# Seven block products, and both halves of an operand in one 512-column matmul, for the MLP up-projection of an encoder block

## The chip, the cores and the metric

The kernel runs on one core of a Trainium2 chip. The metric is the device time of one execution in microseconds (us). The engines in the text are PE (TensorE, with PEld for its weight loads), DVE (VectorE), ACT (ScalarE), POOL (GpSimd) and SP (SyncE, which here issues the DMAs that are not POOL's).

## The reference

All tensors are float32, one batch, 512 tokens, width 2048.

```python
D_MODEL = 2048
SEQ = 512
D_FF = 4 * D_MODEL
...
Block:  h = x + W_out( sig(gA) * P_A(NAtt(xn)) + sig(gB) * P_B(BiGDN(xn)) ),  xn = RMSNorm(x)
        h = h + W_down( relu(RMSNorm(h) W_up)^2 )
        y = RMSNorm_final(h)
```

The change lies in the second of these lines: `W_up` takes the 2048 values of a token to 8192, a relu and a square follow, and `W_down` takes them back to 2048.

## The kernel before, in words

**Arithmetic.** TensorE multiplies in fp32r, a rounded form of float32. So every operand is split in two: `hi` is the value rounded by ACT (a cast, L89 for a weight unit, L94 elsewhere), `lo` is what the rounding left, which DVE subtracts (L90, L95). `unit_mm` then issues three matmuls for each 128x128 piece of a weight: `hi`·`hi` (L115), `hi`·`lo` (L116) and `lo`·`hi` (L117), each over all 512 tokens, so 512 columns.

**Units.** A weight comes in units of 128 partitions by 1024 (512 KB): eight 128x128 pieces that share an output block of 128 rows, for one half of the 2048 inputs. `load_raw` (L82, on SP) brings a unit into one of four `raw` buffers, and `load_unit` splits it into `wh_...` and `wl_...`, three buffers each.

**Stages on PE.** The input projection, the two attention branches and their gates come first. Then come w_out (16 output blocks `m`; `ps_b<-mh,wh_wo` in the trace), the MLP up-projection (64 output blocks of two units; `ps_b<-hh,wh_up`), and the MLP down-projection (`ps_b<-hih,wh_dn`). The last matmuls of the kernel are over 256 columns (L926 to L928).

**The activations of the up-projection.** After each output block of w_out, DVE adds the residual (L855, tile `xr`), ACT and DVE split the result (`hh` L861, `hl` L862), and the sum of its squares goes on (`sqh` L822, `sacc` L826). `stat` and `rstd_bcast` make the reciprocal norm of each token from it: eight one-column matmuls (L833, L834), a row of small DVE instructions (L142, L122 to L127, L145), one matmul. That norm is not applied to `hh` but, as `rB`, at the eviction of the up-projection.

**The up-projection.** For each `m` of 64: two units, 48 matmuls into one PSUM bank; DVE L872 (relu, times `rB`), ACT L873 (square), and SP stores the block to DRAM (`hidD`, L874). From `m` = 41 on, `load_hid` brings eleven finished blocks back (`hr`, L843) and splits them (`hih`, `hil`) for the down-projection. PSUM has seven banks for all of this.

**Order.** The program is written in the order of the stages, but a scheduler places the instructions of each engine by priorities and costs, and each engine works its own queue off in order. Pools give the tiles their buffers: a DMA into a buffer waits until the last reader of the tile before it in that buffer is done, and it waits at the head of SP's queue, with all later DMAs of SP behind it. `big` tiles have 48 buffers of 2 KB, `ev` tiles four.

Of the kernel before, what the change touches and what calls it, by code (L numbers as in the profile page):

```python
# [19 lines left out]
T = 512  # L20
# [7 lines left out]
NPUMP = 4  # L28
# [21 lines left out]
def tile_hybrid_block(  # L50
# [34 lines left out]
    def load_unit(src, name):  # L85
        raw = load_raw(src, name)
        hi = st.tile([128, 1024], F32R, tag="wh", name=f"wh_{name}", bufs=3)
        lo = st.tile([128, 1024], F32R, tag="wl", name=f"wl_{name}", bufs=3)
        S_.copy(out=hi, in_=raw)  # L89
        V.tensor_tensor(out=lo, in0=raw, in1=hi.bitcast(F32), op=ALU.subtract)  # L90
        return hi, lo
# [692 lines left out]
    with ExitStack() as p1:  # L784
# [3 lines left out]
        def bank():  # L788
            return mmp.tile([128, T], F32, tag="mm", name="ps_b")
# [30 lines left out]
        def sumsq(src, m, nm, ts=slice(0, T)):  # L820
            sq = tp.tile([128, T], F32, tag="sq", name=f"sq{nm}", bufs=2)
            S_.activation(out=sq[:, ts], in_=src[:, ts], func=AF.Square)  # L822
            if m == 0:
                V.tensor_copy(out=acc, in_=sq)
            elif m < 15:
                V.tensor_tensor(out=acc[:, ts], in0=acc[:, ts], in1=sq[:, ts], op=ALU.add)  # L826
            return sq
# [15 lines left out]
            nc.sync.dma_start(out=raw, in_=hidD[k])  # L843
            return split(raw, big(f"hih{k}"), big(f"hil{k}"))

        hT = []
        with ExitStack() as p5:
            hq = p5.enter_context(tc.tile_pool(name="hq", bufs=1, side="right", reuse_waits="tile"))
            for m in range(16):
                ps = bank()  # L850
                xr = ev(f"xr{m}")
                nc.sync.dma_start(out=xr, in_=xT[:, m, :])
                for u in range(2):
                    unit_mm(ps, load_unit(wout[m, u], f"wo{m}_{u}"), mix, 8 * u, u == 0, u == 1)
                V.tensor_tensor(out=xr, in0=ps, in1=xr, op=ALU.add)  # L855
                nc.sync.dma_start(out=hTD[m], in_=xr)
                if m < 8:
                    hh, hl = big(f"hh{m}"), big(f"hl{m}")
                else:
                    hh, hl = hq.tile([128, T], F32R, name=f"hh{m}"), hq.tile([128, T], F32R, name=f"hl{m}")  # L860
                S_.activation(out=hh, in_=xr, func=AF.Copy, scale=nlw_s[:, m : m + 1])  # L861
                V.scalar_tensor_tensor(out=hl, in0=xr, scalar=nlw_s[:, m : m + 1], in1=hh.bitcast(F32), op0=ALU.mult, op1=ALU.subtract)  # L862
                hT.append((hh, hl))
                sq = sumsq(xr, m, f"h{m}")
            tasks.append(stat("h", sq))
            hid0 = []
            for m in range(64):
                ps = bank()
                for u in range(2):
                    unit_mm(ps, load_unit(wup[m, u], f"up{m}_{u}"), hT, 8 * u, u == 0, u == 1)  # L870
                r = ev(f"ur{m}")
                V.scalar_tensor_tensor(out=r, in0=ps, scalar=0.0, in1=rB, op0=ALU.max, op1=ALU.mult)  # L872
                S_.activation(out=r, in_=r, func=AF.Square)  # L873
                nc.sync.dma_start(out=hidD[m], in_=r)  # L874
                if m >= 40 and m % 2 == 1 and len(hid0) < 11:
                    hid0.append(load_hid(len(hid0)))

        hp = p1.enter_context(tc.tile_pool(name="hp", bufs=1, side="right", reuse_waits="tile"))
        Ha = hp.tile([128, 16, T], F32, name="Ha")
# [141 lines left out]
```

## Time and profile before

| | |
|---|---|
| time before, median of 2 runs | 2957.06 us (2955.55 to 2958.57) |
| the profiled execution, first to last instruction (its span, and its own time) | 2960.0 us |
| mean granted TensorE clock of that execution | 0.995 |
| busy share of PE, PEld, DVE, ACT, POOL | 98%, 81%, 46%, 29%, 1% |
| PE's first and last start on up-projection matmuls | 1534.5 and 2243.9 us |
| its PE matmuls | 3 x 1024 |

The time of an execution is that of its slowest core, and there is one core. The profiled execution is one more execution than the two timed; durations below are from it. A busy share is an average over the whole span: what an engine does in one stage is read from that stage.

### The profile page before, as it was taken

Reading aid. Unit: us, or ns where it says so; the run is one execution under the profiler, and the core shown is the slowest. Engines: PE = TensorE matmul, PEld = TensorE weight load, DVE = VectorE, ACT = ScalarE, POOL = GpSimd, SP = SyncE. Lnnn points to the kernel's source line nnn. Section 1 sums busy time; section 2 is a strip of 40 time slices with the busy share of each in tenths; the row PEclk is TensorE's granted clock in tenths of the full one; section 3 lists DMA queues with packets and bytes.
Section 4 is the critical chain, followed back from the end, with each engine's and each line's share of the span. In section 5 each row is a group of like instructions: output and inputs, shape, how many; then the busy total and the mean of one; then the engine's idle time right before and its main releaser. Section 6 shows DMA issues by size and latency. Waiting matters only on the chain.

```text
span 2960.0 us, 33906 instructions
## 1 busy us (share of the span) xinstructions
PE 2913.1 (98%) x13432; PEld 2397.5 (81%) x13432; DVE 1365.7 (46%) x2071; ACT 872.6 (29%) x1333; POOL 24.7 (1%) x66
## 2 busy tenths in 40 slices
PE   8999999999999999999999999999999999999998
PEld 6778788888788888888888888888888888888887
DVE  6888769744554443444342222223333242332333
ACT  6444322233233333222222222222223131221322
POOL 0000000000000000000000000000000000000000
PEclk9999999999999999999999999999999999999999
DMA  7556653655532223443433333334336243342322
GB/s 228 185 182 186 207 185 118 219 153 171 183 114 96 91 85 132 160 155 117 148 125 114 123 119 118 120 118 136 128 129 230 94 155 100 107 143 94 113 100 86
DMA packets 170847, 411.95 MB, mean 139 GB/s; under 512 B 34368, under 2 KB 46720, under 8 KB 170688
## 3 DMA queue, kind: packets, MB, share of 16 engines
q1 hardware_dynamic: 170016, 407.69, 41.7%
q0 software_dynamic: 672, 2.10, 0.3%
q8 instruction: 105, 1.72, 0.2%
q14 instruction: 54, 0.44, 0.0%
HBM read 350.84 MB, written 58.88 MB: 138 GB/s over the span
## 4 chain that ended last, share of the span: by engine, by line
PE 72%; DVE 0%; SPq 0%; DMA 0%; ACT 0%; issue 0%; DVEq 0%; POOL 0%
PE ps_b L115 20%; PE ps_b L116 20%; PE ps_b L117 20%; PE ps_mm L117 4%; PE ps_mm L115 3%; PE ps_mm L116 3%; PE ps_ax L676 0%; PE ps_b L926 0%; PE ps_b L927 0%; PE ps_b L928 0%; DVE Ha L906 0%; PE ps_ax L137 0%; PE ps_ax L690 0%; PE ps_ax L692 0%; PE ps_ax L691 0%; PE ps_ax L657 0%
## 5 line engine op out<-in xcount | busy, mean ns | idle before, releaser
L115 PE MATMUL ps_mm<-xh,wh_in 128*128 128x512 f32 x1416 | 567.3, 401 | 3.4 <-ACT wh_in L89 3.4
L117 PE MATMUL ps_mm<-xh,wl_in 128*128 128x512 f32 x1416 | 560.6, 396 | 1.3 <-DVE wl_in L90 1.3
L116 PE MATMUL ps_mm<-xl,wh_in 128*128 128x512 f32 x1416 | 560.0, 395 | 0.0
L115 PE MATMUL ps_b<-hh,wh_up 128*128 128x512 f32 x1024 | 402.0, 393 | 0.0
L117 PE MATMUL ps_b<-hh,wl_up 128*128 128x512 f32 x1024 | 401.7, 392 | 0.0
L116 PE MATMUL ps_b<-hl,wh_up 128*128 128x512 f32 x1024 | 401.5, 392 | 0.0
L116 PE MATMUL ps_b<-hil,wh_dn 128*128 128x512 f32 x992 | 385.8, 389 | 0.0
L117 PE MATMUL ps_b<-hih,wl_dn 128*128 128x512 f32 x992 | 385.7, 389 | 0.0
L115 PE MATMUL ps_b<-hih,wh_dn 128*128 128x512 f32 x992 | 385.7, 389 | 0.0
L117 PEld LDWEIGHTS ps_mm<-xh,wl_in 128*128 128x128 f32 x1416 | 267.8, 189 | 62.3 <-DVE wl_in L90 2.6
L115 PEld LDWEIGHTS ps_mm<-xh,wh_in 128*128 128x128 f32 x1416 | 267.7, 189 | 59.1 <-ACT wh_in L89 4.0
L116 PEld LDWEIGHTS ps_mm<-xl,wh_in 128*128 128x128 f32 x1416 | 267.8, 189 | 54.7 <-issue 0.2
L89 ACT CAST wh_in<-raw_in 128x1024 fp32r<-128x1024 f32 x177 | 186.0, 1051 | 414.5 <-PE ps_mm L116 325.7
L89 ACT CAST wh_up<-raw_up 128x1024 fp32r<-128x1024 f32 x128 | 134.6, 1052 | 529.1 <-PE ps_b L116 300.0
L90 DVE TENSOR_TENSOR wl_up<-raw_up,wh_up 128x1024 fp32r<-128x1024 f32 x128 | 156.8, 1225 | 274.5 <-ACT wh_up L89 274.5
L90 DVE TENSOR_TENSOR wl_in<-raw_in,wh_in 128x1024 fp32r<-128x1024 f32 x177 | 216.2, 1222 | 121.4 <-ACT wh_in L89 114.8
L89 ACT CAST wh_dn<-raw_dn 128x1024 fp32r<-128x1024 f32 x124 | 130.9, 1055 | 477.1 <-PE ps_b L116 461.5
L90 DVE TENSOR_TENSOR wl_dn<-raw_dn,wh_dn 128x1024 fp32r<-128x1024 f32 x124 | 151.9, 1225 | 244.4 <-ACT wh_dn L89 244.1
L116 PEld LDWEIGHTS ps_b<-hl,wh_up 128*128 128x128 f32 x1024 | 192.2, 188 | 43.8 <-issue 0.2
L115 PEld LDWEIGHTS ps_b<-hh,wh_up 128*128 128x128 f32 x1024 | 192.2, 188 | 43.6 <-issue 0.2
L117 PEld LDWEIGHTS ps_b<-hh,wl_up 128*128 128x128 f32 x1024 | 192.1, 188 | 43.4
L116 PEld LDWEIGHTS ps_b<-hil,wh_dn 128*128 128x128 f32 x992 | 186.2, 188 | 38.9 <-DVE hil L95 0.2
(307 smaller groups left out, 3203.1 us busy)
## 6 DMA issues: line engine op xcount, KB each, us to landing
raw_in<-in_win SPq DMA_DIRECT2D x177, 512.0 KB
raw_up<-in_wup SPq DMA_DIRECT2D x128, 512.0 KB
raw_dn<-in_wdn SPq DMA_DIRECT2D x124, 512.0 KB
raw_wo<-in_wout SPq DMA_DIRECT2D x32, 512.0 KB
hidD<-ur SPq DMA_DIRECT2D x64, 256.0 KB
hr<-hidD SPq DMA_DIRECT2D x64, 256.0 KB
gD<-g SPq DMA_DIRECT2D x32, 256.0 KB
raw_pa<-in_wpa SPq DMA_DIRECT2D x16, 512.0 KB
```

The lines of the kernel that those rows point to most:

```text
L89: S_.copy(out=hi, in_=raw)
L90: V.tensor_tensor(out=lo, in0=raw, in1=hi.bitcast(F32), op=ALU.subtract)
L115: PE.matmul(ps, hi[:, w], rh, start=first and kk == 0, stop=False)
L116: PE.matmul(ps, hi[:, w], rl, start=False, stop=False)
L117: PE.matmul(ps, lo[:, w], rh, start=False, stop=last and kk == 7)
```

## The change

The 64 output blocks are taken in 32 pairs (`m0`, `m1` = `m0` + 8), and the weight of a pair is a 2x2 matrix of units: `A11` and `A12` (two halves of the inputs, block `m0`), `A21` and `A22` (block `m1`). The activations are a 2x2 matrix as well: two halves of the inputs by two halves of the tokens, 256 each. The eight block products of such a pair are replaced by seven, of sums and differences of the blocks. `XT1` to `XT4` are made of the activations once, from the differences `TR`; `X11`, `X21`, `X22` are plain blocks. The weight sums are made for every pair: `S1` = `A21` + `A22`, `S3` = `A21` + `A11`, `S2` = `S1` + `A11`, `S4` = `S2` + `A12`.

An activation block of 256 tokens has its `hi` and its `lo` half side by side in one tile of 512 columns. A product is then eight times (one 512-column matmul with the weight's `hi`, one 256-column matmul with its `lo`, L912 and L913). Each half of the bank holds a part of the result, and they are added afterwards on DVE (`fold`, L899; L950 and L955 read both).

`S1` and `S3` are made by DMAs: SP loads `A21` into a `sum` tile (L922, L925), and POOL issues a second DMA that adds the other unit to it (L923, L926, `accum_op`). `S2` and `S4` are DVE additions (L934; L957, and L936 in the first pair). The `sum` tiles have four buffers, and the pool that holds them stands where the `TR` tiles stood before.

```diff
-        hT = []
+        p7 = ExitStack()
+        bq = p7.enter_context(tc.tile_pool(name="bq", bufs=8, side="right", reuse_waits="tile"))
+
+        def operand(src, name):
+            t = bq.tile([128, T], F32R, tag="B2", name=name) if name.startswith("X11") else big(name)
+            split(src, t[:, 0:256], t[:, 256:512])
+            return t
+
+        lo_t, hi_t = slice(0, 256), slice(256, 512)
+        XS = {}
...
+            TR = []
+            xs = []
+            for n, m in enumerate(m for j in range(8) for m in (j, j + 8)):
...
-                if m < 8:
-                    hh, hl = big(f"hh{m}"), big(f"hl{m}")
+                sq = sumsq(xr, n, f"h{m}")
+                S_.activation(out=xr, in_=xr, func=AF.Copy, scale=nlw_s[:, m : m + 1])
+                xs.append(xr)
+                if n % 2 == 0:
+                    XS["11", m] = operand(xr[:, lo_t], f"X11_{m}")
                 else:
-                    hh, hl = hq.tile([128, T], F32R, name=f"hh{m}"), hq.tile([128, T], F32R, name=f"hl{m}")
-                S_.activation(out=hh, in_=xr, func=AF.Copy, scale=nlw_s[:, m : m + 1])
-                V.scalar_tensor_tensor(out=hl, in0=xr, scalar=nlw_s[:, m : m + 1], in1=hh.bitcast(F32), op0=ALU.mult, op1=ALU.subtract)
-                hT.append((hh, hl))
-                sq = sumsq(xr, m, f"h{m}")
+                    j = n // 2
+                    x0, x1 = xs[n - 1], xs[n]
+                    XS["21", j] = operand(x1[:, lo_t], f"X21_{j}")
+                    XS["22", j] = operand(x1[:, hi_t], f"X22_{j}")
+                    t = tr.tile([128, 4, 256], F32, tag="tr", name=f"TR{j}")
+                    V.tensor_tensor(out=t[:, 0], in0=x0[:, lo_t], in1=x0[:, hi_t], op=ALU.subtract)
+                    V.scalar_tensor_tensor(out=t[:, 1], in0=t[:, 0], scalar=-1.0, in1=x1[:, hi_t], op0=ALU.mult, op1=ALU.subtract)
+                    V.tensor_tensor(out=t[:, 2], in0=x1[:, hi_t], in1=x0[:, hi_t], op=ALU.subtract)
+                    V.scalar_tensor_tensor(out=t[:, 3], in0=t[:, 1], scalar=-1.0, in1=x1[:, lo_t], op0=ALU.mult, op1=ALU.subtract)
+                    TR.append(t)
             tasks.append(stat("h", sq))
-            hid0 = []
-            for m in range(64):
-                ps = bank()
-                for u in range(2):
-                    unit_mm(ps, load_unit(wup[m, u], f"up{m}_{u}"), hT, 8 * u, u == 0, u == 1)
-                r = ev(f"ur{m}")
-                V.scalar_tensor_tensor(out=r, in0=ps, scalar=0.0, in1=rB, op0=ALU.max, op1=ALU.mult)
-                S_.activation(out=r, in_=r, func=AF.Square)
-                nc.sync.dma_start(out=hidD[m], in_=r)
-                if m >= 40 and m % 2 == 1 and len(hid0) < 11:
-                    hid0.append(load_hid(len(hid0)))
+            for o, e in (("T2", 1), ("T1", 0), ("T3", 2), ("T4", 3)):
+                for j in range(8):
+                    XS[o, j] = operand(TR[j][:, e], f"X{o}_{j}")
+            def sums(name, bufs=4):
+                return sm.tile([128, 1024], F32, tag="sum", name=name, bufs=bufs)
...
+            def fold(t):
+                V.tensor_tensor(out=t[:, lo_t], in0=t[:, lo_t], in1=t[:, hi_t], op=ALU.add)
+                return t[:, lo_t]
...
+            def product(ps, w, o, first=False):
+                hi, lo = w
+                for j in range(8):
+                    x = XS[o, j]
+                    c = slice(j * 128, (j + 1) * 128)
+                    PE.matmul(ps, hi[:, c], x, start=first and j == 0, stop=False, skip_group_check=True)
+                    PE.matmul(ps[:, 0:256], lo[:, c], x[:, 0:256], start=False, stop=j == 7, skip_group_check=True)
+                    if j % NPUMP == NPUMP - 1:
+                        pump()
+
+            for i in range(32):
+                m0 = i // 8 * 16 + i % 8
+                m1 = m0 + 8
+                a11 = load_raw(wup[m0, 0], f"A11_{i}")
+                s1, s3 = sums(f"S1_{i}"), sums(f"S3_{i}")
+                nc.sync.dma_start(out=s1, in_=wup[m1, 0])
+                G.dma_start(out=s1, in_=wup[m1, 1], accum_op=ALU.add)
+                a12 = load_raw(wup[m0, 1], f"A12_{i}")
+                nc.sync.dma_start(out=s3, in_=wup[m1, 0])
+                G.dma_start(out=s3, in_=wup[m0, 0], accum_op=ALU.add)
+                a22 = load_raw(wup[m1, 1], f"A22_{i}")
+                a, b, c = (bank() for _ in range(3))
+                t1, t5, u2 = et(f"t1_{i}"), et(f"t5_{i}"), et(f"u2_{i}")
+                r0, r1 = ev(f"ur{m0}"), ev(f"ur{m1}")
+                s2, s4 = sums(f"S2_{i}"), sums(f"S4_{i}")
+                product(a, wsplit(a11, f"A11_{i}"), "11", True)
+                S_.copy(out=t1, in_=a)
+                V.tensor_tensor(out=s2, in0=s1, in1=a11, op=ALU.add)
+                if i == 0:
+                    V.tensor_tensor(out=s4, in0=s2, in1=a12, op=ALU.add)
+                    product(c, wsplit(s4, f"S4_{i}"), "22", True)
+                    S_.copy(out=t5, in_=c)
+                    product(a, wsplit(a12, f"A12_{i}"), "21")
+                product(b, wsplit(s2, f"S2_{i}"), "T2", True)
+                V.tensor_tensor(out=u2, in0=b, in1=t1, op=ALU.add)
+                product(c, wsplit(s1, f"S1_{i}"), "T1", i > 0)
+                if i == 0:
+                    V.tensor_tensor(out=t5, in0=c, in1=t5, op=ALU.subtract)
+                else:
+                    S_.copy(out=t5, in_=c)
+                    product(a, wsplit(a12, f"A12_{i}"), "21")
+                f1 = et(f"f1_{i}")
+                S_.copy(out=f1[:, lo_t], in_=a[:, hi_t])
+                V.tensor_tensor(out=f1[:, lo_t], in0=a[:, lo_t], in1=f1[:, lo_t], op=ALU.add)
+                V.scalar_tensor_tensor(out=r0[:, lo_t], in0=f1[:, lo_t], scalar=0.0, in1=rB[:, lo_t], op0=ALU.max, op1=ALU.mult)
+                product(b, wsplit(s3, f"S3_{i}"), "T3")
+                V.tensor_tensor(out=t5, in0=b, in1=t5, op=ALU.add)
+                V.tensor_tensor(out=t5, in0=t5, in1=t1, op=ALU.add)
+                V.scalar_tensor_tensor(out=r1[:, hi_t], in0=fold(t5), scalar=0.0, in1=rB[:, hi_t], op0=ALU.min, op1=ALU.mult)
+                if i > 0:
+                    V.tensor_tensor(out=s4, in0=s2, in1=a12, op=ALU.add)
+                    product(c, wsplit(s4, f"S4_{i}"), "22")
+                V.tensor_tensor(out=u2, in0=c, in1=u2, op=ALU.add)
+                V.scalar_tensor_tensor(out=r0[:, hi_t], in0=fold(u2), scalar=0.0, in1=rB[:, hi_t], op0=ALU.max, op1=ALU.mult)
+                S_.activation(out=r0, in_=r0, func=AF.Square)
+                nc.sync.dma_start(out=hidD[m0], in_=r0)
+                product(b, wsplit(a22, f"A22_{i}"), "T4")
+                V.tensor_tensor(out=t1, in0=b, in1=t1, op=ALU.add)
+                V.scalar_tensor_tensor(out=r1[:, lo_t], in0=fold(t1), scalar=0.0, in1=rB[:, lo_t], op0=ALU.min, op1=ALU.mult)
+                S_.activation(out=r1, in_=r1, func=AF.Square)
+                nc.sync.dma_start(out=hidD[m1], in_=r1)
+            hid0 = [load_hid(k) for k in range(16)]
+        p7.close()
```

The pairs after the first take their products in the order `A11`, `S2`, `S1`, `A12`, `S3`, `S4`, `A22`; the first pair takes `S4` and `A12` right after `A11`. Below, a number behind a tile's name is the pair (and one more that keeps tiles of a name apart).

DVE in the middle of the up-projection, before (the splits of two blocks' units, the eviction of the block before):

```order
L90 TENSOR_TENSOR wl_up20_0_13316<-raw_up20_0_13313,wh_up20_0_13315 128x1024
L90 TENSOR_TENSOR wl_up20_1_13346<-raw_up20_1_13343,wh_up20_1_13345 128x1024
L872 SCALAR_TENSOR_TENSOR ur19_13308<-ps_b_13247,rB_79 128x512
L90 TENSOR_TENSOR wl_up21_0_13381<-raw_up21_0_13378,wh_up21_0_13380 128x1024
L90 TENSOR_TENSOR wl_up21_1_13411<-raw_up21_1_13408,wh_up21_1_13410 128x1024
```

and after, from the addition that makes the next pair's `S2` to the split of that `S2`; `raw_A11`, `wl_A22` and the like are units, `t1`, `t5`, `u2`, `f1` and `ur` are evictions:

```order
L934 TENSOR_TENSOR S2_12_14420<-S1_12_14402,raw_A11_12_14400 128x1024
L95 TENSOR_TENSOR wl_S4_11_14351<-S4_11_14236,wh_S4_11_14350 128x1024
L957 TENSOR_TENSOR S4_12_14421<-S2_12_14420,raw_A12_12_14406 128x1024
L95 TENSOR_TENSOR wl_A22_11_14376<-raw_A22_11_14225,wh_A22_11_14375 128x1024
L950 TENSOR_TENSOR f1_11_14321<-ps_b_14227,f1_11_14321 128x256
L951 SCALAR_TENSOR_TENSOR ur19_14233<-f1_11_14321,rB_79 128x256
L953 TENSOR_TENSOR t5_11_14231<-ps_b_14228,t5_11_14231 128x512
L954 TENSOR_TENSOR t5_11_14231<-t5_11_14231,t1_11_14230 128x512
L95 TENSOR_TENSOR wl_A11_12_14423<-raw_A11_12_14400,wh_A11_12_14422 128x1024
L899 TENSOR_TENSOR t5_11_14231<-t5_11_14231 128x256
L959 TENSOR_TENSOR u2_11_14232<-ps_b_14229,u2_11_14232 128x512
...
L95 TENSOR_TENSOR wl_S2_12_14445<-S2_12_14420,wh_S2_12_14444 128x1024
```

Left out in the last of these are one L955 and one L899, both of 256 columns. What was two splits and an eviction for a block is now seven splits, two additions and thirteen smaller instructions for a pair. The addition that makes `S2` of the next pair (its first operand is the `S1` that a POOL DMA completes) stands right behind this pair's split of `S3`, and ahead of the splits of this pair's `S4` and `A22`.

SP in the same place, before and after (`hidD` is the store of a finished block):

```order
L82 DMA raw_up20_0_13313<-in_wup 128x1024
L82 DMA raw_up20_1_13343<-in_wup 128x1024
L874 DMA hidD_94<-ur17_13178 128x512
L82 DMA raw_up21_0_13378<-in_wup 128x1024
L82 DMA raw_up21_1_13408<-in_wup 128x1024
```

```order
L82 DMA raw_A11_12_14400<-in_wup 128x1024
L82 DMA raw_A12_12_14406<-in_wup 128x1024
L922 DMA S1_12_14402<-in_wup 128x1024
L962 DMA hidD_94<-ur18_14048 128x512
L925 DMA S3_12_14403<-in_wup 128x1024
L967 DMA hidD_94<-ur26_14049 128x512
L82 DMA raw_A22_12_14410<-in_wup 128x1024
L82 DMA raw_A11_13_14585<-in_wup 128x1024
```

The loads of the `sum` tiles are queued between the stores and the other loads. POOL, which issued nothing in this stage before, now has the two adding DMAs of every pair, `S1` then `S3`; each waits for its tile's load, and the second waits behind the first.

The buffers of the `sum` tiles go round: `S1` of a pair takes the one that `S2` of the pair before had, `S2` that of `S3`, `S3` that of `S1`, and `S4` keeps the fourth. So the load of `S1_12` above waits for `wl_S2_11`, the last reader of `S2_11`.

DVE at the end of w_out and the start of the up-projection, before (`xr15` is the last block of w_out, `rsa_h` to `dg_h` the norm):

```order
L855 TENSOR_TENSOR xr15_11913<-ps_b_11912,xr15_11913 128x512
L90 TENSOR_TENSOR wl_up1_0_12081<-raw_up1_0_12078,wh_up1_0_12080 128x1024
L862 SCALAR_TENSOR_TENSOR hl15_11978<-xr15_11913,nlw_s_74,hh15_11977 128x512
L142 TENSOR_SCALAR rsa_h_12012<-ps_s_12002 128x4
...
L145 TENSOR_TENSOR dg_h_12027<-ident_66,rsy_h_12014 128x512
L90 TENSOR_TENSOR wl_up1_1_12111<-raw_up1_1_12108,wh_up1_1_12110 128x1024
L90 TENSOR_TENSOR wl_up2_0_12146<-raw_up2_0_12143,wh_up2_0_12145 128x1024
```

and after, where 32 splits of `XT` tiles (the first and the last are shown) stand ahead of the first sum:

```order
L866 TENSOR_TENSOR xr15_11972<-ps_b_11971,xr15_11972 128x512
L142 TENSOR_SCALAR rsa_h_12194<-ps_s_12184 128x4
...
L145 TENSOR_TENSOR dg_h_12209<-ident_66,rsy_h_12196 128x512
L880 SCALAR_TENSOR_TENSOR TR7_12045<-TR7_12045,xr15_11972 128x256
L95 TENSOR_TENSOR X21_7_12039<-xr15_11972,X21_7_12039 128x256
L95 TENSOR_TENSOR X22_7_12042<-xr15_11972,X22_7_12042 128x256
L881 TENSOR_TENSOR TR7_12045<-xr15_11972,xr7_11900 128x256
L95 TENSOR_TENSOR XT2_0_12050<-TR0_10982,XT2_0_12050 128x256
...
L95 TENSOR_TENSOR XT4_7_12143<-TR7_12045,XT4_7_12143 128x256
L934 TENSOR_TENSOR S2_0_12170<-S1_0_12152,raw_A11_0_12150 128x1024
L936 TENSOR_TENSOR S4_0_12171<-S2_0_12170,raw_A12_0_12156 128x1024
L95 TENSOR_TENSOR wl_S4_0_12223<-S4_0_12171,wh_S4_0_12222 128x1024
```

The splits of the first weights stood there at once before; now the activations' differences, their 32 splits and two sums come between.

## Rows read from the trace of the kernel before

**Rows 1.** The page's chain that ended last, by line.

```profile
PE ps_b L115 20%; PE ps_b L116 20%; PE ps_b L117 20%; PE ps_mm L117 4%; PE ps_mm L115 3%; PE ps_mm L116 3%; PE ps_ax L676 0%; PE ps_b L926 0%; PE ps_b L927 0%; PE ps_b L928 0%; DVE Ha L906 0%; PE ps_ax L137 0%; PE ps_ax L690 0%; PE ps_ax L692 0%; PE ps_ax L691 0%; PE ps_ax L657 0%
```

**Rows 2.** Windows: start:end, length, PE, PEld, DVE, ACT, POOL, PEclk, DMA share, GB/s.

```profile
1534.50:2243.70 709.20, 709.20 (x3090) 578.33 (x3089) 211.26 (x217) 175.78 (x205) 0.00 (x0) 1.00 0.37 123
2300.00:2500.00 200.00, 200.00 (x884) 165.62 (x883) 67.67 (x71) 47.58 (x52) 0.00 (x0) 1.00 0.36 119
```

**Rows 3.** Tile ps_b, up-projection: ns min/median/max, first and last start.

```profile
L115 PE MATMUL ps_b<-hh,wh_up x1024: 389/392/791, 1534.5 to 2243.5; 128*128 128x512 f32 x171
L117 PEld LDWEIGHTS ps_b<-hh,wl_up x1024: 187/188/188, 1534.7 to 2243.7; 128*128 128x128 f32 x171
```

**Rows 4.** Timeline of PE at the kernel's last matmuls: start us, us.

```profile
2918.79 0.39 PE L117 MATMUL ps_b<-hih,wl_dn 128*128 128x512 f32 x1
2919.01 0.28 PE L926 MATMUL ps_b<-hih,wlh 128*128 128x256 f32 x1
2919.13 0.28 PE L927 MATMUL ps_b<-hil,wlh 128*128 128x256 f32 x1
```

**Rows 5.** Timeline of DVE, instructions back to back, in three places.

```profile
1534.66 0.69 DVE L855 TENSOR_TENSOR xr<-ps_b,xr 128x512 f32<-128x512 f32 x1 [3.31 <-PE ps_b L117]
1535.56 1.23 DVE L90 TENSOR_TENSOR wl_up<-raw_up,wh_up 128x1024 fp32r<-128x1024 f32 x1 [0.21 <-ACT wh_up L89]
1536.70 0.75 DVE L862 SCALAR_TENSOR_TENSOR hl<-xr,nlw_s,hh 128x512 fp32r<-128x512 f32 x1
1541.44 0.69 DVE L145 TENSOR_TENSOR dg_h<-ident,rsy_h 128x512 f32<-128x512 f32 x1
...
1211.98 0.69 DVE L814 TENSOR_TENSOR gt<-gt 128x512 f32<-128x512 f32 x1
1212.59 1.22 DVE L90 TENSOR_TENSOR wl_pb<-raw_pb,wh_pb 128x1024 fp32r<-128x1024 f32 x1
...
2943.75 0.41 DVE L931 TENSOR_TENSOR Ha<-ps_b,Ha 128x256 f32<-128x256 f32 x1
2944.08 1.08 DVE L906 TENSOR_TENSOR Ha<-ps_b,Ha 128x256 f32<-128x256 f32 x3
```

**Rows 6.** Timeline of SP, one load of the up-projection.

```profile
1710.68 0.33 SPq L82 DMA_DIRECT2D raw_up<-in_wup  x1
```

**Rows 7.** Windows around that load; DMA share and GB/s stand last.

```profile
1711.00:1712.00 1.00, 1.00 (x6) 0.82 (x5) 0.00 (x0) 0.00 (x0) 0.00 (x0) 1.00 0.39 57
1712.00:1713.00 1.00, 1.00 (x6) 0.78 (x6) 0.00 (x0) 0.00 (x0) 0.00 (x0) 1.00 0.88 315
1713.00:1714.00 1.00, 1.00 (x6) 0.82 (x5) 0.00 (x0) 0.07 (x1) 0.00 (x0) 1.00 0.38 152
```

**Rows 8.** POOL's DMAs of 512 KB (L466), by line.

```profile
L466 POOLq EVENT_SEMAPHORE  x3: 17/43/43, 362.5 to 372.8; - x3
L466 POOL DMA_DIRECT2D MT<-Nd x2: 1050/1050/1050, 373.3 to 374.4; - x2
...
DMA to landing us min/median/max: 11.5/12.7/14.0
```

**Rows 9.** POOL's DMAs of 128 KB (L472), by line.

```profile
L472 POOL DMA_DIRECT2D sf<-Nd x8: 648/648/812, 361.7 to 400.9; - x8
...
DMA to landing us min/median/max: 2.9/8.5/15.0
```

**Rows 10.** The DMA engines from 373 to 388 us, by queue: packets, MB, share.

```profile
q1 hardware_dynamic: 1300, 2.89, 60.1%
q0 software_dynamic: 383, 1.34, 41.4%
```

**Rows 11.** Timeline of PE behind a gap near the kernel's start.

```profile
36.14 0.50 PE L115 MATMUL ps_mm<-xh,wh_in 128*128 128x512 f32 x1 [3.42 <-ACT wh_in L89]
38.00 0.63 PE L115 MATMUL ps_mm<-xh,wh_in 128*128 128x512 f32 x1
```

**Rows 12.** ACT from 2243 to 2270 us, where down follows up.

```profile
L94 ACT CAST hih<-hr 128x512 fp32r<-128x512 f32 x7 | 4.2, 619 | 4.0 <-DMA hr<-hidD 3.9
```

More of the change, by code (lines that the diff above doesn't have):

```diff
@@ L844, in load_hid @@
             return split(raw, big(f"hih{k}"), big(f"hil{k}"))
-        hT = []
+        p7 = ExitStack()
[6 more added lines that the diff above has]
+        XS = {}
         with ExitStack() as p5:
-            hq = p5.enter_context(tc.tile_pool(name="hq", bufs=1, side="right", reuse_waits="tile"))
-            for m in range(16):
+            tr = p5.enter_context(tc.tile_pool(name="tr", bufs=8, side="right", reuse_waits="tile"))
+            TR = []
+            xs = []
+            for n, m in enumerate(m for j in range(8) for m in (j, j + 8)):
                 ps = bank()
@@ new lines, in tile_hybrid_block, with et, wsplit @@
+            tasks.append(stat("h", sq))
+            for o, e in (("T2", 1), ("T1", 0), ("T3", 2), ("T4", 3)):
+                for j in range(8):
+                    XS[o, j] = operand(TR[j][:, e], f"X{o}_{j}")
+        with ExitStack() as p6:
+            sm = p6.enter_context(tc.tile_pool(name="sm", bufs=1, side="right", reuse_waits="tile"))
+            def sums(name, bufs=4):
+                return sm.tile([128, 1024], F32, tag="sum", name=name, bufs=bufs)
+            def et(name):
+                return sm.tile([128, T], F32, tag="et", name=name, bufs=6)
+            def fold(t):
+                V.tensor_tensor(out=t[:, lo_t], in0=t[:, lo_t], in1=t[:, hi_t], op=ALU.add)
+                return t[:, lo_t]
+            def wsplit(raw, name):
+                hi = st.tile([128, 1024], F32R, tag="wh", name=f"wh_{name}", bufs=3)
+                lo = st.tile([128, 1024], F32R, tag="wl", name=f"wl_{name}", bufs=3)
+                return split(raw, hi, lo)
+            def product(ps, w, o, first=False):
[59 more added lines that the diff above has]
+            hid0 = [load_hid(k) for k in range(16)]
```

## The prediction

> **What bounds the kernel now.** I read the page's chain first: its three largest entries, 60% of the span, are the three matmul lines on `ps_b`, which is w_out, up and down [rows 1]. The kernel is bound by PE wherever it runs such stages. Then the stage itself: over the 709.2 us of the up-projection PE is busy for 709.2, while DVE works 211, ACT 176, and the DMA engines are at 0.37 [rows 2]. So what this stage costs is its matmul columns, and every other engine has more than half of its time left. In the down-projection 884 matmuls of 512 columns start in 200 us, one each 0.2262 us [rows 2]. A weight load takes 0.188 us [rows 3], hidden beside the matmul ahead of it. At the end of the kernel, 256-column matmuls start 0.12 us apart (2919.01 to 2919.13), each with a new weight [rows 4].
>
> **What PE gains.** A pair of blocks was 96 matmuls of 512 columns. It becomes seven products of eight (512 + 256) columns: 56 x (0.2262 + 0.120) = 19.39 us, and 32 pairs are 620 us. The stage was 709.2, so 89 us less; about 2 us of the 709.2 are the norm's own small matmuls, which stay. I take **87**. The low end is 75, if all that the stage has above 3072 x 0.2262 = 695 us stays.
>
> **What DVE and ACT get.** Back to back on DVE, a 1024-column instruction starts 1.14 us before the next (1535.56 to 1536.70), a 512-column one 0.61, a 256-column one 0.33 [rows 5]. A pair has 9 x 1.14 + 5 x 0.61 + 8 x 0.33 = 16.0 us of them, below PE's 19.4. ACT has seven casts and some evictions, less than DVE. Neither is the bound by its sum. What they do is hidden behind PE, but only while nothing on DVE waits.
>
> **The wait that the change adds.** The load of `S1` needs the buffer of the last pair's `S2`, so it can't be issued before DVE has split that. Then POOL adds `A22` to it, and the DVE addition that makes the next `S2` waits for that. Behind this addition on DVE stand `wl_S4` and `wl_A22` of the pair that PE is working on, so PE waits too, after the `S3` product. From that addition to the split of `S2` DVE has 14 instructions: six of 1024 columns, three of 512, five of 256, or 5 x 1.14 + 1.23 + 3 x 0.61 + 5 x 0.33 = 10.4 us. Only one of them waits for PE, L959 for the `S4` product, which starts behind `wl_S4` and takes 2.8 us; DVE comes to it 7 us after `wl_S4`. Then the buffer is free again. This is a loop, and its length P is the time of a pair if it is above 19.4:
>
> P = 10.4 (DVE) + 3.4 (load of `S1`) + X (the adding DMA, from the load's landing to its own) = 13.8 + X.
>
> The 3.4 is from one load of the same size: issued at 1710.68 [rows 6], its 524 KB (57 + 315 + 152 GB/s, each for 1 us) moved from 1711 to 1714 [rows 7], and 0.1 for SP's start. PE is the bound only while X is below 5.6 us.
>
> **What X is.** No row shows an adding DMA. The nearest are POOL's plain ones. Between the semaphore that POOL waited for (372.8) and the issue (373.3) lie 0.5 us; the issue took 1.05 and the landing came 11.5 to 14.0 us later, for 512 KB [rows 8]. That was beside SP's transfers on full engines: the two queues had 60% and 41% of them [rows 10]. A quarter of that size, 128 KB, took 0.65 to issue and at best 2.9 us to land [rows 9].
> - Low end: 0.5 + 2.9 + 0.4 (longer issue) + three quarters of the 2.3 us in which the load above moved its bytes (1.7) = 5.5 us. P = 19.3, and PE is the bound.
> - High end: 0.5 + 12.7 = 13.2 us. P = 27.0.
> - What I take: behind `S1` SP issues the load of `S3`, then `A22`, within a few us, and POOL's queue must share the engines with them. The bytes of the adding DMA then take twice 2.3 us: 0.5 + 2.9 + 0.4 + 4.6 - 0.6 (the quarter that is in the 2.9) = **7.8 us, P = 21.6**. The engines' mean load speaks for a place near the low end: per pair 7 x 0.52 MB of loads and 2 x 0.26 MB of stores in 19.4 us are 216 GB/s, a share of 0.65 by the stage's 0.37 at 123 [rows 2], where the 11.5 to 14.0 were measured at full engines.
>
> The Trainium skill, page "Collectives: The Full Stack", section "The bandwidth ceiling: the fold count and why AG ≠ RS ≠ AR", says that an adding transfer has to read two sources and so delivers at half the rate of a copy. By that, X would be about 7.8 us without any contention and more with it. No row here shows whether it does.
>
> **The start.** Before, the first up-projection matmul follows w_out with no gap. Now only `A11` of the first pair (2.8 us) can. The next product needs `S4`, which is made of `S2` and so of `S1`, whose buffer lies where the last `TR` tile was. On DVE: the norm ended at 1541.44 + 0.69 in the trace, with a weight split and `hl` ahead of it that now come later [rows 5], so I put its end at 1541.5; five instructions on the last block (1.7) and 32 splits of 256 columns (10.6) bring 1553.8. ACT's casts of the same tiles run ahead of DVE. Then the load (3.4), X (6.5, between the low end and the value taken, since the loads of two sums run together), `S2` and `S4` on DVE (2.4) and the cast of `S4` on ACT (1.05): 1567.1. PE had matmuls up to 1534.5 + 2.8 + some 2 for the norm = 1539.3, so it is idle for 28 us. A gap of 3.4 us was followed by 512-column matmuls that took 0.63 instead of 0.39 us [rows 11], a few of them; a gap of 28 us will cost as much, 1 to 2 us. I take **+29**; 24 to 34 by X.
>
> **The end.** All 16 blocks for the first part of the down-projection are now loaded behind the loop, where eleven had been there. `hr2` stands on SP behind the store of the last block: eviction, fold, multiplication on DVE, square on ACT (0.61 + 0.33 + 0.33, and 0.62 as for a cast of this size: 1.9), two issues (0.33 each), a load (up to 3.3), a cast (0.62 [rows 12]), 6.5 us. PE has 12 matmuls, 2.7 us, on `hr0` and `hr1`. That leaves 3.8 us; the trace shows 3.9 us of waiting for such loads at this place already, on ACT [rows 12]. Later loads wait for one of four `ev` buffers. I take **+5**, bounds 3 and 10.
>
> **The sum.** On the profile's scale: 2960.0 - 87 + 29 + 5 = 2907, plus 31 x (P - 19.4). The profiled execution is 3 us above the median of the two runs, so 2904 + 31 x (P - 19.4). With P = 21.6: 2904 + 68 = **2972 us**, +0.5%. The clock doesn't add to that: a pair has 2.2 us of idle PE time, and if PE is slower for a while behind it, the loop, in which PE has no part, still sets the pair's time.
>
> **The rivals.**
> 1. *A cheap addition.* X is at its low end or below it, and PE is never waited for: 2904 us, 1.8% faster. For it: the engines' load of 0.65, and the 2.9 us of the quarter-size DMA. Against it: SP's loads come just when POOL's DMA runs. The Trainium skill, page "DMA: Bandwidth & Descriptors", section "Anatomy of one DMA — SWDGE (gpsimd) path", gives for a POOL DMA 2.0 us plus the bytes at 436 GB/s; an estimate from it is 3.2 us for 512 KB, so X = 3.7. The 11.5 us and more of the trace disagree with it, on busy engines.
> 2. *A dear addition*, which is slower than before. X is near what the trace shows for 512 KB from POOL. At 10.5 us, half way from 7.8 to 13.2, P = 24.3 and the time is 3056; at 13.2, 3140. It decides from 2% above the median (3016): 31 x (P - 19.4) = 112, P = 23.0, X = 9.2. For it: the only rows of this size [rows 8], and that an addition reads its destination too. Against it: they were taken with the engines full.
> 3. *The paired matmul is bound by its weight load.* If each 256-column matmul were as long as the load of its weight, 0.188 us, a pair would take 56 x 0.414 = 23.2 us, and the time would be 2904 + 32 x 3.8 = 3026. Against it stand three rows: loads of 0.188 us lie beside matmuls 0.12 us apart [rows 3, 4].
> 4. *A cheaper start*, as if the sums were there when the splits are done: 10 us off any of these; with rival 1 it is the only way to over 2% faster.
>
> **How the numbers follow.** Chances: forecast (X from 6.5 to 9.2, 2930 to 3016) 0.47; rival 1 without the cheaper start (2895 to 2930) 0.20; rival 2 0.21; rival 3 0.04; rival 4 with rival 1 0.08. A measurement of this kernel tells about 2% from no change, 2898 to 3016. Faster by over 2%: 0.08. Slower: rivals 2 and 3, with a little of the forecast's edge, 0.26. The rest, 0.66, is within. The range leaves out the 0.08 below and rival 2's dearer half: 2896 to 3060. The likeliest case by itself is 2930 to 3016.
>
> **What the profile after would show.** Right: products of 2.77 us, a 256-column matmul handing over to the next after 0.12; once a pair, ahead of the `S4` product, PE idle for about 2 us, released by `wl_S4` or `wh_S4`, with DVE's addition L934 waiting for the DMA of `S1`; pairs 21 to 22 us apart; POOL's L923 landing 6.5 to 8 us after its issue starts; one gap of 25 to 30 us near 1540; some us of waiting for `hr` where the down-projection starts. Wrong: no idle time in a pair (rival 1), L923 landing beyond 9 us (rival 2), products of 3.3 us without a wait (rival 3). I would also be wrong if another wait closed a longer loop than this one, for instance if SP's queue, with stores and loads in a fixed order, held `S1` back behind a block that isn't evicted yet.

## The result, and the profile after

The changed kernel took 3031.3 us (median of two, 3027.7 to 3034.9) against 2957.1: a ratio of 1.025, interval 1.022 to 1.028. That is slower by 2.5%, where 2972 us and +0.5% were forecast. The profiled execution has a span of 3033.0 us, 73.0 more than before. By stage: w_out ends 2.4 us later, which varies from kernel to kernel (over those below, that end lies between 1525 and 1537); from there to the first matmul of the down-projection it is 63.6 us more (1536.6 to 2310.2, where it was 1534.2 to 2244.2); from there to the end 7.0 more.

The page's chain after, by engine and by line, beside [rows 1]:

```profile
PE 68%; DMA 14%; DVE 13%; issue 4%; ACT 1%; SPq 0%; DVEq 0%; POOLq 0%; ACTq 0%
PE ps_b L115 11%; PE ps_b L117 11%; PE ps_b L116 11%; DMA S<-in_wup 9%; PE ps_mm L116 8%; PE ps_mm L115 8%; PE ps_mm L117 8%; PE ps_b L912 3%; DVE wl_S L95 3%; DVE wl_A L95 2%; PE ps_b L913 2%; DVE wl_in L90 1%; DMA gB<-rowD 1%; DMA bB<-rowD 1%; DMA XQ<-Nd 1%
```

Before, no line but PE's matmuls had 1% of it. Now 9% of the span is the DMA into the `sum` tiles (`S<-in_wup`) and 5% the splits `wl_S` and `wl_A` on DVE. Windows of the up-projection after, beside [rows 2]:

```profile
1700.00:2200.00 500.00, 440.67 (x2410) 373.94 (x2411) 359.53 (x481) 210.56 (x258) 36.77 (x42) 0.99 0.67 180
```

PE works 441 of 500 us here, DVE 360, and no engine is full. The waits of 1540 to 2300 us (us in total, times, longest) name the link between them:

```profile
DVE S L934 <- DMA S<-in_wup: 190.6, 32, 10.2
PE ps_b L913 <- DVE wl_S L95: 55.8, 30, 3.4
PE ps_b L912 <- ACT wh_S L94: 54.1, 26, 28.0
```

All 32 additions that make `S2` (L934) waited for the DMA that completes `S1`, 6 us each, and PE waited for what stands behind them on DVE. One turn of that loop, in timelines of DVE, SP and POOL:

```profile
1813.53 1.23 DVE L934 TENSOR_TENSOR S<-S,raw_A 128x1024 f32<-128x1024 f32 x1 [5.28 <-DMA S<-in_wup]
1814.67 1.22 DVE L95 TENSOR_TENSOR wl_S<-S,wh_S 128x1024 fp32r<-128x1024 f32 x1
1815.92 1.22 DVE L957 TENSOR_TENSOR S<-S,raw_A 128x1024 f32<-128x1024 f32 x1
1818.20 0.42 DVE L950 TENSOR_TENSOR f<-ps_b,f 128x256 f32<-128x256 f32 x1
1818.65 0.42 DVE L951 SCALAR_TENSOR_TENSOR ur<-f,rB 128x256 f32<-128x256 f32 x1
1818.99 0.68 DVE L953 TENSOR_TENSOR t<-ps_b,t 128x512 f32<-128x512 f32 x1
1819.71 0.69 DVE L954 TENSOR_TENSOR t<-t,t 128x512 f32<-128x512 f32 x1
1823.06 1.22 DVE L95 TENSOR_TENSOR wl_S<-S,wh_S 128x1024 fp32r<-128x1024 f32 x1
...
1801.29 0.33 SPq L922 DMA_DIRECT2D S<-in_wup  x1
1824.31 0.33 SPq L922 DMA_DIRECT2D S<-in_wup  x1
...
1805.69 0.88 POOL L923 DMA_DIRECT2D S<-in_wup  x1 [18.94 <-DVE wl_A L95]
```

Read it from SP: the load of `S1` goes out at 1801.29; POOL issues the adding DMA at 1805.69 (4.40 later); the addition on DVE starts when it has landed, at 1813.53 (7.84 later); the split of `S2` begins at 1823.06 and the next load of `S1` goes out at 1824.31 (10.78 later). The sum is 23.02 us, and the next pair starts over. From the second load of `S1` (1570.80) to the last (2266.91) they go out every 23.2 us in the mean. In each of the 31 turns the load goes out 0.03 us after a split `wl_S` ends, and from the third turn on it is 10.77 or 10.78 us behind the addition: the link through the buffer closes in every pair. The adding DMAs of `S1`, by line:

```profile
L923 POOL DMA_DIRECT2D S<-in_wup x32: 866/875/967, 1560.1 to 2271.2; - x32
DMA to landing us min/median/max: 5.7/7.9/8.9
```

The start and the end, in timelines of SP, POOL and PE (the numbers in brackets are idle time and what ended it):

```profile
1555.80 0.33 SPq L922 DMA_DIRECT2D S<-in_wup  x1
1560.13 0.97 POOL L923 DMA_DIRECT2D S<-in_wup  x1 [439.21 <-DMA S<-in_wup]
...
1569.57 0.80 PE L912 MATMUL ps_b<-X,wh_S 128*128 128x512 f32 x1 [28.02 <-ACT wh_S L94]
...
2302.16 0.28 PE L913 MATMUL ps_b<-XT,wl_S 128*128 128x256 f32 x1
2302.52 0.28 PE L913 MATMUL ps_b<-X,wl_S 128*128 128x256 f32 x1
...
2310.16 0.73 PE L115 MATMUL ps_b<-hih,wh_dn 128*128 128x512 f32 x2 [2.06 <-ACT hih L94]
2317.04 1.22 PE L115 MATMUL ps_b<-hih,wh_dn 128*128 128x512 f32 x2 [3.17 <-ACT hih L94]
```

PE is idle for 28.0 us ahead of the first `S4` product; the two DMAs of the first `S1`, from 1555.80 to the addition on DVE at 1565.95, are 10.2 of them. At the end it waits 2.1 and 3.2 us for `hr` blocks. The two rows between, both 256-column matmuls, stand 0.36 us apart, with a 512-column one in between.

### The profile page after: what moved, and what is told of

It is laid out like the page before. It is cut to its first block, busy times and chain, and to the rows that moved or that the text cites. A ratio compares the mean times of both kernels' runs of the same rounds, so it can differ in the third digit from the quotient of the medians.

```text
span 3033.0 us, 36231 instructions
## 1 busy us (share of the span) xinstructions
PE 2868.6 (95%) x13944; PEld 2380.8 (78%) x13944; DVE 1715.7 (57%) x2656; ACT 1039.6 (34%) x1581; POOL 81.0 (3%) x130
## 4 chain that ended last, share of the span: by engine, by line
PE 68%; DMA 14%; DVE 13%; issue 4%; ACT 1%; SPq 0%; DVEq 0%; POOLq 0%; ACTq 0%
PE ps_b L115 11%; PE ps_b L117 11%; PE ps_b L116 11%; DMA S<-in_wup 9%; PE ps_mm L116 8%; PE ps_mm L115 8%; PE ps_mm L117 8%; PE ps_b L912 3%; DVE wl_S L95 3%; DVE wl_A L95 2%; PE ps_b L913 2%; DVE wl_in L90 1%; DMA gB<-rowD 1%; DMA bB<-rowD 1%; DMA XQ<-Nd 1%
## 5 line engine op out<-in xcount | busy, mean ns | idle before, releaser
L912 PE MATMUL ps_b<-XT,wh_S 128*128 128x512 f32 x768 | 275.6, 400 | 1.9 <-DVE u L941 1.9
L94 ACT CAST wh_S<-S 128x1024 fp32r<-128x1024 f32 x128 | 134.3, 1049 | 296.5 <-PE ps_b L912 232.5
L115 PEld LDWEIGHTS ps_b<-hih,wh_dn 128*128 128x128 f32 x992 | 186.4, 188 | 45.7 <-ACT hih L94 7.1
L117 PEld LDWEIGHTS ps_b<-hih,wl_dn 128*128 128x128 f32 x992 | 186.6, 188 | 38.3
L913 PE MATMUL ps_b<-XT,wl_S 128*128 128x256 f32 x768 | 216.3, 282 | 0.0
L912 PE MATMUL ps_b<-X,wh_A 128*128 128x512 f32 x512 | 183.2, 396 | 0.0
L912 PEld LDWEIGHTS ps_b<-XT,wh_S 128*128 128x128 f32 x768 | 145.0, 189 | 38.3 <-ACT wh_A L94 2.2
L95 DVE TENSOR_TENSOR wl_S<-S,wh_S 128x1024 fp32r<-128x1024 f32 x128 | 155.9, 1218 | 13.3 <-ACT wh_S L94 13.3
```

What stands on the lines that cost most here:

```text
L94: S_.copy(out=hi, in_=src)
L95: V.tensor_tensor(out=lo, in0=src, in1=hi.bitcast(F32), op=ALU.subtract)
L115: PE.matmul(ps, hi[:, w], rh, start=first and kk == 0, stop=False)
L117: PE.matmul(ps, lo[:, w], rh, start=False, stop=last and kk == 7)
L912: PE.matmul(ps, hi[:, c], x, start=first and j == 0, stop=False, skip_group_check=True)
L913: PE.matmul(ps[:, 0:256], lo[:, c], x[:, 0:256], start=False, stop=j == 7, skip_group_check=True)
```

## The experiments

**The loop, cut by two more buffers (e1).**

```diff
-            def sums(name, bufs=4):
+            def sums(name, bufs=6):
```

> The changed kernel with six buffers for the sum tiles instead of four, so that the load of S1 no longer waits for the split of the last pair's S2; the scheduler also moves the addition that makes S2 to another place on DVE. My theory (a loop of S2's addition, S2's split, S1's load and the adding DMA sets the pair's time of 23.2 us): the loop is cut and PE sets the time. In the profile after, a 512- and a 256-column matmul take 0.354 us together, so a pair is 56 x 0.354 = 19.8 us, and 3031 - 31 x (23.2 - 19.8) = 2926 us, up to 10 less if the first S1 comes earlier too. Rival (the adding DMAs or the DMA engines themselves can't do a pair faster; two landings of 7.9 and 7.1 us and 0.67 of the engines' time are in a pair now): the pair stays above 22 us and the time above 2990 us.

Measured: 2919.7 us (2911.3 to 2923.8; ratio to the kernel before 0.986, 0.984 to 0.988). It is within the first theory's range and 112 us below the changed kernel, with the same products, the same DMAs and the same additions. Windows of the stage:

```profile
1700.00:2100.00 400.00, 400.00 (x2269) 347.61 (x2268) 332.64 (x447) 195.52 (x243) 34.95 (x40) 1.00 0.78 214
```

PE is busy for all 400 us; the DMA share rose to 0.78, since the same transfers come in less time. So neither the adding DMAs nor the DMA engines had set the pair's time by themselves: the loop through the buffer had. The scheduler moved the addition on DVE as well, so this run alone does not part the buffer from the order; that the load waited for its buffer in every pair is shown by the trace of the changed kernel. The start's idle time fell from 28.0 to 17.8 us: the load of the first `S1` went out at 1536.85 and no longer behind the `XT` splits.

**What the addition costs (e2).** POOL's two DMAs as plain copies:

```diff
-                G.dma_start(out=s1, in_=wup[m1, 1], accum_op=ALU.add)
+                G.dma_start(out=s1, in_=wup[m1, 1])
...
-                G.dma_start(out=s3, in_=wup[m0, 0], accum_op=ALU.add)
+                G.dma_start(out=s3, in_=wup[m0, 0])
```

> The changed kernel with POOL's two DMAs of a pair as plain copies of the same size (leaves out the additions that make S1 and S3); the order and all waits stay. If the addition itself is dear (its bytes took the DMA engines 1.7 times as long as SP's, 5.6 against 3.3 us per MB in the stretch 1800 to 1826): the landing of S1's DMA falls from 7.9 to about 5.5 us, the pair from 23.2 to 20.8, the time to 3031 - 31 x 2.4 = 2957. Rival (it is POOL's queue and the sharing with SP's loads that take the time): landing still above 7 us, time above 3000.

Measured: 2975.6 us (2971.4 to 2980.7), between the two. The landing of `S1`'s DMA:

```profile
L923 POOL DMA_DIRECT2D S<-in_wup x32: 537/537/582, 1554.5 to 2209.3; - x32
DMA to landing us min/median/max: 3.8/6.0/7.0
```

The addition costs 1.9 us of the 7.9 in landing, which is counted from the start of POOL's issue; the issue itself is 0.34 shorter. 31 x 1.9 = 59 us agrees with 3031.3 - 2975.6 = 55.7. So the theory holds in kind, and was one third too large (74 us). POOL's queue from 1700 to 2100 us, with the adding DMAs and with the plain ones:

```profile
q0 software_dynamic: 4910, 17.86, 24.2%
q0 software_dynamic: 5357, 19.49, 14.1%
```

That is 5.42 against 2.89 us of the engines per MB, 1.87 times. The Trainium skill says of the adding step of a reduce-scatter that it needs two source reads and so has half the rate of a copy ("Collectives: The Full Stack", "The bandwidth ceiling: the fold count and why AG ≠ RS ≠ AR"); the 1.87 of this trace is near it.

**What runs beside it (e3, e9).** First without `S3`'s adding DMA (line L926 left out), then without `S3`'s load too (ACT copies `A22` into the tile instead):

```diff
-                nc.sync.dma_start(out=s3, in_=wup[m1, 0])
-                G.dma_start(out=s3, in_=wup[m0, 0], accum_op=ALU.add)
...
+                S_.copy(out=s3, in_=a22)
```

> The changed kernel without the adding DMA of S3 (leaves out that addition; S3's load stays, S1's adding DMA too). If S1's DMA is slow because S3's runs beside it from some 3 us after its start: landing from 7.9 to about 6.5, the pair to 21.8, the time to 3031 - 43 = 2988. If only SP's loads beside it count, or nothing beside it: landing as before within 0.4 us, time above 3015.

> The changed kernel with neither of S3's two DMAs (leaves out that sum: ACT copies A22 into the tile instead); four sum buffers, and S1's load and adding DMA as they were. The run without S3's adding DMA alone changed nothing, so if S1's adding DMA is slowed by what shares the engines with it, it is SP's load of S3, which starts 2 us after S1's and so lies under the adding DMA: landing from 7.9 to about 6 us, the pair from 23.2 to 21.3, 3031 - 59 = 2972 us. Rival (nothing shares to speak of, and an adding DMA of this size takes that long by itself): landing above 7.4, time above 3015.

Measured: 3034.9 us (3031.4 to 3038.4) without the second addition, the same as with it, and a landing of 8.0: my theory of that run fell. Without both, 2968.8 us (2965.2 to 2973.5), the time that I had expected, but not by the way that I had expected. One turn there, in timelines of DVE, SP and POOL (the addition that makes `S2` is L933 here):

```profile
1815.57 1.23 DVE L933 TENSOR_TENSOR S<-S,raw_A 128x1024 f32<-128x1024 f32 x1 [2.40 <-DMA S<-in_wup]
1824.05 1.22 DVE L95 TENSOR_TENSOR wl_S<-S,wh_S 128x1024 fp32r<-128x1024 f32 x1
...
1804.05 0.33 SPq L922 DMA_DIRECT2D S<-in_wup  x1
1825.29 0.33 SPq L922 DMA_DIRECT2D S<-in_wup  x1
...
1808.10 0.87 POOL L923 DMA_DIRECT2D S<-in_wup  x1 [20.08 <-DVE wl_A L95]
```

4.05 + 7.47 + 9.72 = 21.24 us. Against the turn above, the load is 0.35 shorter and the adding DMA 0.37; the other 1.06 us are DVE's, where the split of `S4` now stands ahead of the addition and no longer inside the loop. So `S3`'s transfers cost the loop 0.7 us in this turn (0.9 in the mean from the second turn on), not 2.

What is left is not all the adding DMA's own. SP's stores and its loads of `A` units still lie beside it here: in the turn shown SP's queue had 36.5% of the engines between POOL's issue and the addition. The first pair parts the two, because SP moves nothing beside its POOL DMA. In the changed kernel, the queues from POOL's issue of `S1` to the addition on DVE, in the first pair and in the turn shown above:

```profile
q0 software_dynamic: 193, 0.73, 72.3%
q1 hardware_dynamic: 2, 0.00, 0.0%
...
q0 software_dynamic: 190, 0.71, 53.3%
q1 hardware_dynamic: 400, 1.18, 47.2%
```

The landing of that first DMA, adding in the changed kernel and plain in the run with plain copies (where SP's queue had 0.1% beside it):

```profile
S<-in_wup POOLq DMA_DIRECT2D x1, 512.0 KB, 5.7
...
S<-in_wup POOLq DMA_DIRECT2D x1, 512.0 KB, 3.8
```

With SP's transfers beside it the medians are 7.9 and 6.0. So of the 7.9 us a plain DMA alone is 3.8, the addition 1.9, and what SP moves beside it 2.2; the 2.2 is the same with and without the addition.

**The sums on DVE, without POOL (e4).**

```diff
-                G.dma_start(out=s1, in_=wup[m1, 1], accum_op=ALU.add)
+                a22 = load_raw(wup[m1, 1], f"A22_{i}")
+                V.tensor_tensor(out=s1, in0=s1, in1=a22, op=ALU.add)
...
+                V.tensor_tensor(out=s3, in0=s2, in1=a22, op=ALU.subtract)
                 product(b, wsplit(s3, f"S3_{i}"), "T3")
```

> The seven products with no POOL DMA: A21 is loaded into a sum tile, DVE adds A22 to it (S1), and S3 is made by DVE as S2 - A22 (the same sum by another way); six sum buffers. Loads of a pair fall from seven to four units, DVE gets two more instructions of 1024 columns, 18.3 us of a pair by their starts. My theory: PE sets the pair, 19.8 us, and the start is shorter by most of S1's 7.9 + 4: 3031 - 105 - 10 = 2916 us. Rival (DVE, with its waits on ACT and PE in a fixed order, becomes the bound): a pair of 21 us or more, 2955 and above.

Measured: 2916.1 us (2913.5 to 2919.4; ratio 0.985, 0.984 to 0.987). Windows:

```profile
1700.00:2100.00 400.00, 400.00 (x2268) 347.52 (x2267) 377.07 (x486) 195.40 (x243) 0.00 (x0) 1.00 0.41 134
```

DVE works 377 of 400 us and PE still never waits in this stretch. The DMA share is 0.41. The time is that of six buffers with POOL's DMAs (2911.3 to 2923.8) to within their spread, so once the loop is cut, the place where the sums are made is not seen in the time.

**The start (e5, e8).** The first pair written apart, with the splits between its products:

```diff
+            a11, a12, a22, s1 = (load_raw(wup[m, u], f"{n}_0") for m, u, n in ((0, 0, "A11"), (0, 1, "A12"), (8, 1, "A22"), (8, 0, "S1")))
...
+            V.tensor_tensor(out=s1, in0=s1, in1=a22, op=ALU.add)
+            V.tensor_tensor(out=s2, in0=s1, in1=a11, op=ALU.add)
+            product(a, wsplit(a11, "A11_0"), "11", True)
...
+            V.tensor_tensor(out=a12, in0=s2, in1=a12, op=ALU.add)
+            product(c, wsplit(a12, "S4_0"), "22", True)
...
+            xt("T2", 1)
+            product(b, wsplit(s2, "S2_0"), "T2", True)
```

> e4 with the first pair written apart: its four units are raw tiles, its S1, S2 and S4 are made from them in place before w_out ends, its S4 and A12 products come right behind A11, and the splits of the XT tiles stand between its products. In e4 PE is idle for 19 us there, and the whole pair ends some 24 us after w_out's end and its 19.8 us of matmuls. My theory of the start (PE waits for 32 splits and two sums on DVE that stand in front of the first sum): DVE has 10.6 for the splits, 8 for seven weight splits, 3.4 for three sums and some 5 for evictions, 27 us, beside 19.8 us of PE, so about 8 to 11 us come back: 2906 us. Rival (the norm's chain and the last block of w_out hold all of it, or the second pair's sums, which can only be loaded when the TR tiles are free, take it back): less than 4 us, 2912 and above.

> e5 with two more edits: 12 of the 32 XT subtractions on POOL, and two thirds of the first 16 hidden blocks staged in two other buffers instead of the ev ones. From e4: 9 us for the first pair, 3 for the splits that DVE no longer has, 5 of the 9 us where the down-projection starts: 2916 - 17 = 2899, a ratio to the kernel before of 0.980. Rival (POOL's subtractions and DVE's hold each other up, or the hidden blocks are bound by the DMA engines at 0.8 to 0.9 there): 2906 and above.

Measured: 2901.2 us (2898.7 to 2910.3) for the first pair alone, 15 below the run with the sums on DVE and more than I had expected. With POOL's share of the splits and the other staging it is 2898.4 us (2897.1 to 2899.1), a ratio of 0.980 (0.978 to 0.981): the time expected, though the last two edits gave 3 us together and not 8, and 3 us lie within the spread of the run with the first pair alone.

**The order of the widths, and all together (e6, e10).**

```diff
+                for j in range(8):
+                    PE.matmul(ps, hi[:, j * 128 : (j + 1) * 128], XS[o, j], start=first and j == 0, stop=False, skip_group_check=True)
...
+                for j in range(8):
+                    PE.matmul(ps[:, 0:256], lo[:, j * 128 : (j + 1) * 128], XS[o, j][:, 0:256], start=False, stop=j == 7, skip_group_check=True)
```

> e4 with the eight 512-column matmuls of a product first and the eight 256-column ones behind them, instead of in turns. A 512- and a 256-column matmul take 0.353 us in turns in e4, where 0.226 and 0.120 = 0.346 were measured in rows of one kind. If it is the turn from one width to the other that costs: 1792 x 0.0065 = 12 us come back, 2904 us. Rival (the operands' reads cost, whatever the order): 2916 within 4 us.

> The run with the first pair written apart, POOL's share of the splits and the other staging, and in addition the products with their eight 512-column matmuls first. The order of the matmuls gave 10 us beside the sums on DVE; if that adds up: 2898 - 10 = 2888 us, a ratio to the kernel before of 0.976. Rival (the gain came from the start, where wl is needed later, which the new first pair has already): 2894 and above.

Measured: 2906.4 us (2906.2 to 2909.6) with the sums on DVE, 10 less, and 2900.6 us (2896.7 to 2904.0) on top of the last version, 2 more. The windows of the first of the two:

```profile
1700.00:2100.00 400.00, 400.00 (x2291) 351.34 (x2290) 379.17 (x493) 200.22 (x244) 0.00 (x0) 1.00 0.39 135
```

2291 matmuls start in 400 us where 2268 did: 0.349 us for the two widths and not 0.353. That is 6 us over the stage, half of what I expected, so the turn from width to width is about half of the excess. The rest of the 10 us lies ahead of the stage: in the profiled executions w_out ends 3.8 us earlier. The same 2291 stand in the last run, but there PE waits 6.6 us for the second pair's `S2`, where the version without this edit waited 0.5. Two numbers of this size can't be told from the runs' own spread.

**The end by itself (e7)**, on the kernel before:

```diff
-                if m >= 40 and m % 2 == 1 and len(hid0) < 11:
-                    hid0.append(load_hid(len(hid0)))
```

> The kernel before without the early loads of eleven hidden blocks in the up-projection: all 16 are loaded behind it. This is the end cost by itself. My theory of the end (PE waits for hr loads that stand behind the last store and for the four ev buffers): 5 to 9 us more, 2965 to 2969. Rival (the wait of 9 us that the changed kernel shows there comes from its sums and evictions, not from the missing early loads): within 2 us of 2959.6.

Measured: 2976.5 us (2972.7 to 2978.8), 18 more than the kernel before had beside it (2958.6), outside both. In timelines of PE and SP:

```profile
2253.80 0.79 PE L115 MATMUL ps_b<-hih,wh_dn 128*128 128x512 f32 x1 [16.86 <-ACT hih L94]
...
2238.74 8.60 SPq L880 DMA_DIRECT2D Ha<-hTD  x14
2247.70 2.35 SPq L843 DMA_DIRECT2D hr<-hidD  x4
```

The scheduler put all 16 loads of `Ha` (4 MB; two stand ahead of the rows shown) on SP ahead of the first `hr`, and PE waited 16.9 us. In the changed kernel the `hr` loads stand between those of `Ha`. So this run shows a price of an order on SP, and does not measure the wait that was meant.

## Why the prediction came out as it did

**What bounds it, and the loop.** Right, and shown twice over: in the trace by the 32 waits of L934, and by the first experiment, where two more buffers took PE's waits away and 112 us with them. The size was too small: 3031 lies inside the range, but 15 us above the likeliest case's own. The forecast of +0.5% was no clear change by its own words (0.66); slower had 0.26, and slower is what came.

**The mis-sized term is P**, the length of the loop: 21.6 us forecast, 23.0 in the turn shown and 23.2 over all. Its three parts were all a little short, and none was left out. The turn shown:

| part of the loop | forecast | measured |
|---|---|---|
| DVE, from the addition to the next load's issue | 10.4 | 10.78 |
| the load and POOL's start (3.4 + 0.5) | 3.9 | 4.40 |
| the adding DMA, issue to landing | 7.3 | 7.84 |

The means from the second turn on are 10.83, 4.70 and 7.67. On DVE I had added the distances of instructions that don't read each other. The rows after show longer ones where one does: 0.45 us for L950 to L951 and not 0.33, 0.72 for L953 to L954 and not 0.61; and L957 starts 1.25 after the split ahead of it and not 1.14. It reads what L934 wrote two instructions ahead, but L899 reads what L954 wrote two ahead and starts at 1.14 (1820.32 to 1821.46), so the cause of this one stays open. The load was timed on engines at 0.37 of their time, and they are at 0.67 now. The excess, 31 x 1.6 = 50 us, is nearly all of the 59 that the forecast lacks.

**X.** Of 8.3 us (with POOL's start) I had 7.8, and part of that is luck. From issue to landing the forecast had 5.0 us for a plain DMA alone (2.9 + 0.4 + 1.7), nothing for the addition, and 2.3 for sharing the engines with SP. The runs give 3.8, 1.9 and 2.2. So the sharing was right, and 47.2% of the engines did go to SP in the turn shown; the addition was put at nothing in the sum, and a plain DMA priced 1.2 too dear made up for most of it. Rival 2 was said to decide from X = 9.2; the time crossed that line at X near 8.3 because the rest of the loop was 0.9 longer.

**PE's gain.** It was forecast as 87 us. In the runs without waits in the middle of the stage a pair takes 56 x 0.353 = 19.8 us and not 19.4, so it is 709.2 - 32 x 19.8 less the norm's 2, about 74, at the low end that was given. In the changed kernel that hardly shows, since PE has no part in the loop. Rival 3 is ruled out: 0.353 us for the two widths, not 0.414.

**The start** was forecast as 28 us of idle time and was 28.0. The two DMAs of `S1` are 10.2 of it (9.9 forecast), and with six buffers, where they run beside the splits, 10.2 are gone. With the sums on DVE the gap is 19.0, and with the first pair written apart as well none there is longer than 1.6 us, so the rest was the place of the splits and sums. **The end** was +5, with bounds 3 and 10: 7.0 beyond the first down matmul and 2.1 ahead of it, 9 in all. The mechanism (waits for `hr`) is in the rows; why it is 9 and not 5 stays open, since the run made for it measured something else.

**Rival 1** would have been right of the DMA alone only at X below 5.6; the least landing of an adding DMA in these runs was 5.4 us, with POOL's start of 0.5 on top, so not even an adding DMA alone is that cheap. The estimate from the Trainium skill's figure ("DMA: Bandwidth & Descriptors", "Anatomy of one DMA — SWDGE (gpsimd) path"), 3.2 us for a POOL DMA of this size, was undercut by no run: the plain one of `S1` landed after 3.8 us alone and 6.0 in the median, beside SP's loads, and the least of all plain ones of this size there was 3.7.

## What to carry to other kernels

When a change adds a load that waits for a buffer, write down the loop from the buffer's release through load, landing and use back to the release, and hold its length against the bound engine's time: here 23 us against 19.8, with no engine more than 90% busy, and two more buffers (4 KB per partition each), with the order on DVE that came with them, were worth 112 us. An error of half a microsecond in a loop counts once per turn, so take each link from rows under the load that the changed kernel will have, and each distance between instructions that read each other from such a pair. What the block products saved in matmuls (about 74 us here) was less than what the making of their first operands (28), the end (9) and the loop (105) took away. With the loop cut and the start rewritten the same products take 2898.4 us, a ratio of 0.980 to the kernel before; the interval leaves open whether that is more than 2%. Price a new kind of transfer by its parts, alone, with its own extra work, and beside what else moves: here 3.8, 1.9 and 2.2 us.

## What the runs showed of the hardware that was not expected

- An adding DMA of 512 KB from POOL landed 5.4 to 10.4 us after its issue in this stage, a plain one in the same place 3.7 to 7.0; with nothing from SP beside them 5.7 and 3.8. POOL's issue took 0.875 against 0.537 us.
- The plain DMAs of 512 KB of [rows 8] had landed after 11.5 to 14.0 us. They come from another tensor and took 1.05 us to issue, so the difference is not shown to be that of the full engines alone.
- A 512-column and a 256-column matmul in turns take 0.353 us together, in blocks of eight 0.349, and 0.346 by rows of one width each.
- In these rows, a DVE instruction that reads what the one right ahead wrote starts 0.11 to 0.12 us later than one that doesn't: 0.45 and 0.72 us above for 256 and 512 columns, and 1.25 (1551.66, 1552.91, 1554.17) for the first three sums of 1024 in the run with the sums on DVE, where 0.33, 0.61 and 1.14 were read before.
